# A two-layer decoder trunk on one core: projection weights split into a high and a low part by DMA

## The chip, the cores and the metric

The kernel runs on one core of a Trainium2 chip. The metric is device time in microseconds of that core, lower is better; a separate profiled execution gives the trace from which the engines' work is read. The engines are PE (matmuls), PEld (its weight loads), DVE (VectorE), ACT (ScalarE), POOL (GpSimd) and SP (SyncE, which here only issues DMAs).

## The reference

Two layers, each a pre-norm mixer, on a sequence of 1024 rows of width 1024, all in float32:

```python
for l in range(DEPTH):                                  # 2
    ada = silu(c) @ w_ada[l] + b_ada[l]
    shift, scale, gate = jnp.split(ada, 3, axis=-1)
    h = rmsnorm(x, norm_g[l]) * (1.0 + scale[:, None, :]) + shift[:, None, :]
    p = h @ w_in[l]                                     # 1024 x 9224
    mq, mk, mv, mo, mz, mi, mf, rq, rk, rv, rz = split_cols(p)
    ...
    y = jnp.concatenate([y_m, y_r], axis=-1) @ w_out[l] # y_m, y_r: 4 mLSTM and 4 retention heads of 256
    x = x + gate[:, None, :] * y
return rmsnorm(x, final_g)
```

Most of the arithmetic is the product with w_in: 72 column groups of 128 (and eight gate columns) per layer, then the product with w_out.

## The kernel before, in words

**Three products for one.** A float32 operand is held as two float32r tiles, a rounded high part and the rest, the low part. Each product is three matmuls, high x high, high x low and low x high (`mm3`, lines 145 to 147). Every operand therefore has to be split: `split_to` (lines 621 and 622) lets ACT copy the tile into the high part, which rounds it, and then an engine (POOL unless another is named) subtracts the high part from the tile and writes the low part.

**The projections.** `hT` holds the normalised input, transposed, split, in 8 groups of 128 rows of k and two halves of 512 columns of the sequence. `proj_units` (line 363) does one 128-column projection in four units: for each half of the sequence, k 0 to 3 and then k 4 to 7, 12 matmuls each; after a half its PSUM bank is evacuated by ACT and DVE. `v_path` (line 579) does the 256 columns of a head's v in eight row tiles, each of which runs through all eight k. `load_w` (line 353) brings the weights: `load_w_raw` (line 338) has SP issue a DMA of 256 KB into a `raw` tile of 128 x 512 (four k of 128 columns, or two k of 256), and `split_w` (line 348) splits it into a `wH` and a `wL` tile. A 128-column projection takes two such blocks, a v takes four. The `raw` tiles share four buffers, `wH` and `wL` six each.

**What does not go through `load_w`.** The first three projections of each layer (`first`, line 1194) have their own loads: in layer 0 tiles of another pool, in layer 1 `load_w_raw` and `split_w` (line 1187). The v of head 0 and the gate columns (`v0_raw`, line 419, and `v0_split`) load eight raw tiles of 128 x 256 per layer through the same four `raw` buffers. In layer 0 four of these loads are issued before the hand-written order of the first stage (`script`, line 1208) begins, and each of the others when the split of the tile four before it has been written down. The output stage (`OutLoads`, line 955) draws w_out in 64 pieces per layer through `raw`, `wH` and `wL`, and with them the normalised head outputs (`yr`) and the gates (`gr`). The adaLN sums draw w_ada through `raw` too (`ada_rows`, line 254).

**What sets the order.** PE runs in the order in which the program is written, and so does every engine in the first stage of layer 0. Elsewhere a planner orders each engine's queue at build time, by its own estimate of when an instruction can start; on the chip each queue is run strictly in that order. While the projections run, `tick` (line 124) advances generators that write the attention of earlier heads between units of projections: scores (split into `sH` and `sL`, the low part by POOL), values, state updates, and the normalisation, whose power -0.5 is taken by POOL (lines 899 and 904).

Of the kernel before, what the change touches and what calls it, by code (L numbers as in the profile page):

```python
# [77 lines left out]


@with_exitstack  # L80
def tile_hybrid_trunk(ctx, tc, x, xt, c, positions, w_ada, b_ada, norm_g, w_in, conv_w, conv_b,
                      b_igate, b_fgate, gn_m, gn_r, w_out, final_g, consts, out):
    nc = tc.nc
    V, A, G, PE, Q = nc.vector, nc.scalar, nc.gpsimd, nc.tensor, nc.sync
# [169 lines left out]
    def ada_rows(l, c0, accs):  # L254
        acc = bt()
        accs.append(acc)
        prev = None
        for k in range(KT + 1):
            raw = None
            if k < KT:  # L260
                raw = wt("raw", 512, 4)
                Q.dma_start(raw, w_ada[l, k * P:(k + 1) * P, c0:c0 + 512])
            if k == 1:
                V.tensor_scalar(acc, prev, cact[:, 0:1], None, ALU.mult)
            elif k > 1:
# [18 lines left out]
    def gate_rows(l, res):  # L284
        for half in range(2):
            accs = []
            yield from ada_rows(l, 2 * D + half * 512, accs)
            brow = wt("th", 512, 5)
            Q.dma_start(brow[0:1, :], b_ada[l, 2 * D + half * 512:2 * D + (half + 1) * 512].unsqueeze(0))
            yield 1  # L290
            acc = accs[0]
            V.tensor_tensor(acc[0:1, :], acc[0:1, :], brow[0:1, :], ALU.add)
            yield 1
            a2 = (wt("wH", 512, 6, F32R), wt("wL", 512, 6, F32R))
# [40 lines left out]
            V.tensor_scalar(hf, pt, gsh[l][:, 0, k:k + 1], gsh[l][:, 1, k:k + 1], ALU.mult, ALU.add)  # L335
        return hf

    def load_w_raw(src, c0, n):
        kk = 512 // n
        raws = []  # L340
        for p in range(KT // kk):
            raw = wt("raw", 512, 4)
            Q.dma_start(raw.rearrange("p (a b) -> p a b", a=kk),
                        src[p * kk * P:(p + 1) * kk * P, c0:c0 + n].rearrange("(a p) b -> p a b", p=P))
            raws.append(raw)
            yield raw

    def split_w(raw, n, eng=G):
        wH, wL = wt("wH", 512, 6, F32R), wt("wL", 512, 6, F32R)
        split_to((wH, wL), raw, eng)  # L350
        return [(wH[:, a * n:(a + 1) * n], wL[:, a * n:(a + 1) * n]) for a in range(512 // n)]

    def load_w(src, c0, n):
        res = []
        for raw in load_w_raw(src, c0, n):
            res += split_w(raw, n)
        return res

    def half_block(pt, w, hT, half, k0, k1):
# [57 lines left out]
        return gr  # L417

    def v0_raw(l, k):
        raw = wt("raw", 512, 4)[:, 0:HD]  # L420
        Q.dma_start(raw, w_in[l, k * P:(k + 1) * P, OFF_MV:OFF_MV + HD])
        return raw

# [143 lines left out]
    def ocol(hg, m):  # L567
        return OFF_MO + hg * HD + m * P

    def gate_path(l, hg, hT, res, m0=0, m1=2, z0=True):  # L570
        for m in range(m0, m1):
            if m or z0:
                w = load_w(w_in[l], zcol(hg, m), P)
                yield from proj_units(w, hT, z_evac(res, m, None if hg < 4 else gdr[l][hg]))
            if hg < 4:
                w = load_w(w_in[l], ocol(hg, m), P)
                yield from proj_units(w, hT, o_evac(res, m, gdr[l][hg]))

    def v_path(l, hg, hT, gt, vs):
        h, ml = hg % 4, hg < 4  # L580
        w = load_w(w_in[l], (OFF_MV if ml else OFF_RV) + h * HD, HD)
        for half in range(2):
            for jj in range(2):
                j = half * 2 + jj
                pt = ps_p()
                for tt in range(2):
                    o = pt[:, tt * HD:(tt + 1) * HD]
                    ts = slice(jj * CH + tt * P, jj * CH + (tt + 1) * P)
                    for k in range(KT):
                        mm3(o, (hT[k][half][0][:, ts], hT[k][half][1][:, ts]), w[k], k == 0, k == KT - 1)  # L590
                    if tt == 0:
                        yield
                vs.append(v_split(hg, gt, pt, j))
                yield
# [85 lines left out]

    def qk_ml(l, hg, which, hT, gt, kt, res):
        for m in range(2):
            w = load_w(w_in[l], (OFF_MK if which else OFF_MQ) + hg * HD + m * P, P)
            halo = wt("halo", 3, 2)

            def evac(half, pt):
                acc = conv_silu(l, hg, which, m, half, pt, halo)
                if not which:
                    q_split(acc, res[m], half)
                    return  # L690
                t2 = (bt(F32R), bt(F32R))
                split_to(t2, acc)
                res[m][half] = t2
                k_store(acc, l, hg, m, half)
                if m:
                    for j in ((0, 1), (2,))[half]:
                        launch(k_rows(l, hg, j, kt, gt), 1)

            yield from proj_units(w, hT, evac)

    def qk_ret(l, h, which, hT, kt, res, cosT, sinT):
        base = (OFF_RK if which else OFF_RQ) + h * HD
        su = []

        def evac0(half, p0):
            s, u = wt("acc", 512, 4), wt("acc", 512, 4)
            V.tensor_tensor(s, p0, cosT[half], ALU.mult)
            V.tensor_tensor(u, p0, sinT[half], ALU.mult)
            su.append((s, u))

        def evac1(half, p1):
            s, u = su[half]
            a, b = wt("th", 512, 5), wt("th", 512, 5)
            V.tensor_tensor(a, p1, sinT[half], ALU.mult)
            V.tensor_tensor(b, p1, cosT[half], ALU.mult)
            V.tensor_tensor(s, s, a, ALU.subtract)  # L716
            V.tensor_tensor(u, u, b, ALU.add)
            for m, src in ((0, s), (1, u)):
                if not which:
# [10 lines left out]
        w = load_w(w_in[l], base, P)  # L730
        yield from proj_units(w, hT, evac0)
        w = load_w(w_in[l], base + P, P)
        yield from proj_units(w, hT, evac1)

    def load_rotary(rot):
# [219 lines left out]
    class OutLoads:  # L955
# [3 lines left out]

        def stage(self, n=1):  # L960
            for half, cc, k in self.todo[:n]:
                raw = wt("raw", 512, 4)
                Q.dma_start(raw, w_out[self.l, k * P:(k + 1) * P, cc * 512:(cc + 1) * 512])
                wH, wL = wt("wH", 512, 6, F32R), wt("wL", 512, 6, F32R)
# [217 lines left out]
    for l in range(DEPTH):  # L1182
# [1 line left out]
        gp = [[None, None], [None, None]]  # L1184
        wf = [[], [], []]
        if l > 0:
            gens = [load_w_raw(w_in[l], col, P) for col in (zcol(0, 0), ocol(0, 0), zcol(0, 1))]
# [18 lines left out]
        if l == 0:  # L1206
# [10 lines left out]
            for step in script.split():  # L1217
# [55 lines left out]
                        vrw.append(v0_raw(0, n + 4))  # L1273
                elif what == "W":
                    i, p = arg
                    wsp[i, p] = wt("wH", 512, 6, F32R), wt("wL", 512, 6, F32R)
# [25 lines left out]
        run_units(proj_units(load_w(w_in[l], ocol(0, 1), P), hT, o_evac(gp, 1, gdr[l][0])))  # L1302
        gp1 = [[None, None], [None, None]]
        run_units(proj_units(load_w(w_in[l], zcol(1, 0), P), hT, z_evac(gp1, 0)))
        gb = []
        gcol = gsh[0][:, 0, :]
        for hg in range(8):
# [65 lines left out]
        hT = nhT  # L1373


_INS = ['x', 'xt', 'c', 'positions', 'w_ada', 'b_ada', 'norm_g', 'w_in', 'conv_w', 'conv_b', 'b_igate', 'b_fgate',
        'gn_m', 'gn_r', 'w_out', 'final_g']
_OUTS = [((1, T, D), 'float32')]

# [23 lines left out]
```

## Time and profile before

| what | value |
|---|---|
| device time, median of 2 runs | 2300.2 us (2299.34 to 2301.05) |
| profiled execution, span from first to last instruction | 2298.7 us |
| PE busy | 2269.4 us, 12411 matmuls |
| DVE busy | 1338.7 us |
| ACT busy | 926.5 us |
| POOL busy | 827.5 us |
| bytes moved by DMA | 259.45 MB, 39.8% of the 16 DMA engines' span |
| mean granted clock | 0.999 |

The profile gives the span of the profiled execution, and no time around it; the two timed runs lie 0.6 and 2.4 us above the span. Busy time is the sum of instructions of an engine; the issuing of DMAs is not counted in it. A row of a group of instructions names line, engine, operation, output and inputs, shapes and count, then busy time and mean length in ns, then how long the engine stood idle just before them and what ended most of that. A row of the timeline gives start, length, engine, line, operation and count. A row of a stretch gives length, the busy time of PE, PEld, DVE, ACT and POOL with their instruction counts, the granted clock, the DMA share and GB/s. A row of waits gives who waited for whom, the total, how often, and the longest.

### The profile page before, as it was taken

How to read it: one execution, taken by the hardware profiler on the slowest of the kernel's cores; microseconds unless marked ns; L12 is line 12 of the kernel's file. 1: busy time of each engine (PE TensorE's matmuls, PEld its weight loads, DVE VectorE, ACT ScalarE, POOL GpSimd, SP SyncE). 2: the span in 40 equal slices, each digit the busy share in tenths (PEclk: the TensorE clock that was granted, in tenths of full speed). 3: DMA queues.
4: the chain of work that ended last, by engine and by line, in shares of the span. 5: the costliest groups of instructions: out<-in, count | busy, mean ns of one | idle time of the engine just before them, and what ended most of it. 6: DMA issues, size and time to landing. Idle time of an engine off the chain costs nothing. (4 is left out here: it accounts for less than half of the span.)

```text
span 2298.7 us, 34322 instructions
## 1 busy us (share of the span) xinstructions
PE 2269.4 (99%) x12411; PEld 1953.7 (85%) x12411; DVE 1338.7 (58%) x2821; ACT 926.5 (40%) x1785; POOL 827.5 (36%) x820
## 2 busy tenths in 40 slices
PE   7999999999999999999999999999999999999998
PEld 5888888889988888988888889888898898988886
DVE  7467688556555555585435676555564545556563
ACT  7535433444332323343544454444343323234442
POOL 0343333333333334224562434333334334341313
PEclk9999999999999999999999999999999999999999
DMA  8333333324433533476532323233223233436674
GB/s 258 80 69 94 83 80 82 83 70 115 124 110 87 149 96 79 126 254 212 169 105 67 84 71 82 77 77 79 68 71 98 74 91 88 124 84 205 184 242 125
DMA packets 360246, 259.45 MB, mean 113 GB/s; under 512 B 113266, under 2 KB 297338, under 8 KB 360076
## 3 DMA queue, kind: packets, MB, share of 16 engines
q1 hardware_dynamic: 359932, 257.00, 39.8%
q8 instruction: 97, 1.59, 0.3%
q14 instruction: 73, 0.60, 0.1%
q10 hardware_dynamic: 144, 0.26, 0.0%
HBM read 201.57 MB, written 55.61 MB: 112 GB/s over the span
## 5 line engine op out<-in xcount | busy, mean ns | idle before, releaser
L145 PE MATMUL pp<-b,wH 128*128 128x512 f32 x1824 | 719.6, 395 | 0.0
L146 PE MATMUL pp<-b,wH 128*128 128x512 f32 x1824 | 718.6, 394 | 0.0
L147 PE MATMUL pp<-b,wL 128*128 128x512 f32 x1824 | 717.6, 393 | 0.0
L622 POOL TENSOR_TENSOR wL<-raw,wH 128x512 fp32r<-128x512 f32 x338 | 453.9, 1351 | 542.3 <-ACT wH L621 478.7
L147 PEld LDWEIGHTS pp<-b,wL 128*128 128x128 f32 x1824 | 342.5, 188 | 80.4
L145 PEld LDWEIGHTS pp<-b,wH 128*128 128x128 f32 x1824 | 342.7, 188 | 73.1 <-DVE g L550 0.3
L146 PEld LDWEIGHTS pp<-b,wH 128*128 128x128 f32 x1824 | 342.5, 188 | 72.1 <-issue 0.2
L621 ACT CAST wH<-raw 128x512 fp32r<-128x512 f32 x402 | 245.7, 616 | 310.8 <-PE pp L146 109.9
L145 PE MATMUL pp<-wH,b 128*128 128x256 f32 (+1 forms) x1024 | 303.0, 296 | 0.0
L147 PE MATMUL pp<-wH,b 128*128 128x256 f32 (+1 forms) x1024 | 301.9, 295 | 0.0
L146 PE MATMUL pp<-wL,b 128*128 128x256 f32 (+1 forms) x1024 | 301.9, 295 | 0.0
L622 POOL TENSOR_TENSOR b<-acc,b 128x256 fp32r<-128x256 f32 (+1 forms) x192 | 176.6, 939 | 299.0 <-ACT b L621 287.7
L146 PEld LDWEIGHTS pp<-wL,b 128*128 128x128 f32 x1024 | 192.9, 188 | 5.8
L145 PEld LDWEIGHTS pp<-wH,b 128*128 128x128 f32 x1024 | 192.4, 188 | 6.0 <-DVE g L550 0.3
L147 PEld LDWEIGHTS pp<-wH,b 128*128 128x128 f32 x1024 | 192.7, 188 | 5.7
L639 DVE SCALAR_TENSOR_TENSOR acc<-pp,cols,acc 128x511 f32<-128x511 f32 (+2 forms) x192 | 142.4, 742 | 40.7 <-ACT acc L634 38.8
L621 ACT CAST b<-acc 128x256 fp32r<-128x256 f32 (+1 forms) x192 | 83.8, 476 | 180.7 <-DVE acc L716 129.3
L622 POOL TENSOR_TENSOR sL<-th,sH 128x256 fp32r<-128x256 f32 (+1 forms) x62 | 57.9, 934 | 207.7 <-ACT sH L621 161.9
L643 ACT ACTIVATE th<-acc 128x512 f32<-128x512 f32 x64 | 40.5, 632 | 145.7 <-DVE acc L641 77.9
L621 ACT CAST cH<-cf 128x516 fp32r<-128x516 f32 (+1 forms) x80 | 49.8, 622 | 105.8 <-DVE va L903 55.7
L622 DVE TENSOR_TENSOR wL<-raw,wH 128x512 fp32r<-128x512 f32 x64 | 44.3, 694 | 62.5 <-ACT wH L621 58.7
L145 PE MATMUL pa<-b,b 128*128 128x256 f32 (+1 forms) x256 | 72.3, 283 | 1.8 <-DVE th L787 1.0
(297 smaller groups left out, 3639.2 us busy)
## 6 DMA issues: line engine op xcount, KB each, us to landing
raw<-in_w_in_dram SPq DMA_DIRECT2D x274, 256.0 KB
raw<-in_w_out_dram SPq DMA_DIRECT2D x128, 256.0 KB
gdr<-g SPq DMA_DIRECT2D x64, 256.0 KB
ndr<-zt SPq DMA_DIRECT2D x128, 128.0 KB
raw<-in_w_ada_dram SPq DMA_DIRECT2D x64, 256.0 KB
g<-gdr SPq DMA_DIRECT2D x64, 256.0 KB
acc<-ndr SPq DMA_DIRECT2D x64, 256.0 KB
acc<-kdr SPq DMA_DIRECT2D x192, 64.0 KB
```

The source lines that it names most:

```text
L145: PE.matmul(o, lt[0], rt[0], start=start, stop=False)
L146: PE.matmul(o, lt[0], rt[1], start=False, stop=False)
L147: PE.matmul(o, lt[1], rt[0], start=False, stop=stop)
L621: A.copy(dst[0], src)
L622: eng.tensor_tensor(dst[1], src, f(dst[0]), ALU.subtract)
L639: V.scalar_tensor_tensor(acc[:, d:], pt[:, 0:HALF - d], wcol, acc[:, d:], ALU.mult, ALU.add)
L643: A.activation(th, acc, AF.Tanh, scale=0.5)
```

## The change

`load_w` no longer brings a raw tile. For each block POOL issues a DMA from w_in's block straight into `wH`, a float32r tile, so that the DMA rounds; ACT writes the negated `wH` into `wL`; and POOL issues a second DMA from the same block that adds to `wL`. The result in `wL` is the weight less its high part. The subtraction on POOL and the cast on ACT go for these blocks. For that the host lays w_in out a second time: `w_blk` with 72 column groups, each as two contiguous blocks of 128 x 512, and `w_val` with the v columns of eight heads, each as four. `load_w_raw` (now only for the start of layer 1) reads those blocks as well, still by SP. `wH` and `wL` get seven buffers instead of six, `raw` two instead of four. The loads of w_out, w_ada and the v of head 0 are as they were, but share the two `raw` buffers.

```diff
-                raw = wt("raw", 512, 4)
+                raw = wt("raw", 512, 2)
...
-    def load_w_raw(src, c0, n):
-        kk = 512 // n
-        raws = []
-        for p in range(KT // kk):
-            raw = wt("raw", 512, 4)
-            Q.dma_start(raw.rearrange("p (a b) -> p a b", a=kk),
-                        src[p * kk * P:(p + 1) * kk * P, c0:c0 + n].rearrange("(a p) b -> p a b", p=P))
-            raws.append(raw)
+    def w_block(l, c0, n, p):
+        if n == P:
+            return w_blk[l, (c0 - 8 * (c0 > OFF_I)) // P, p]
+        return w_val[l, (c0 - OFF_MV) // HD if c0 < OFF_I else NH + (c0 - OFF_RV) // HD, p]
+
+    def load_w_raw(l, c0, n):
+        for p in range(KT * n // 512):
+            raw = wt("raw", 512, 2)
+            Q.dma_start(raw, w_block(l, c0, n, p))
             yield raw
 
     def split_w(raw, n, eng=G):
-        wH, wL = wt("wH", 512, 6, F32R), wt("wL", 512, 6, F32R)
+        wH, wL = wt("wH", 512, 7, F32R), wt("wL", 512, 7, F32R)
         split_to((wH, wL), raw, eng)
         return [(wH[:, a * n:(a + 1) * n], wL[:, a * n:(a + 1) * n]) for a in range(512 // n)]
 
-    def load_w(src, c0, n):
+    def load_w(l, c0, n):
         res = []
-        for raw in load_w_raw(src, c0, n):
-            res += split_w(raw, n)
+        for p in range(KT * n // 512):
+            wH, wL = wt("wH", 512, 7, F32R), wt("wL", 512, 7, F32R)
+            G.dma_start(wH, w_block(l, c0, n, p))
+            A.activation(wL, f(wH), AF.Copy, scale=-1.0)
+            G.dma_start(wL, w_block(l, c0, n, p), accum_op=ALU.add)
+            res += [(wH[:, a * n:(a + 1) * n], wL[:, a * n:(a + 1) * n]) for a in range(512 // n)]
         return res
...
     def v0_raw(l, k):
-        raw = wt("raw", 512, 4)[:, 0:HD]
+        raw = wt("raw", 512, 2)[:, 0:HD]
...
+    cols = _np.concatenate([w[:, :, :OFF_I], w[:, :, OFF_I + 8:]], 2).reshape(DEPTH, 2, 4, P, 72, P)
+    vals = _np.concatenate([w[:, :, OFF_MV:OFF_MV + 1024], w[:, :, OFF_RV:OFF_RV + 1024]], 2)
+    laid = {'xt': inputs['x'][0].T, 'w_blk': cols.transpose(0, 4, 1, 3, 2, 5).reshape(DEPTH, 72, 2, P, 512),
+            'w_val': vals.reshape(DEPTH, 4, 2, P, 8, HD).transpose(0, 4, 1, 3, 2, 5).reshape(DEPTH, 8, 4, P, 512)}
```

More of the change, by code (lines that the diff above doesn't have):

```diff
@@ L80, in tile_hybrid_trunk @@
 @with_exitstack
-def tile_hybrid_trunk(ctx, tc, x, xt, c, positions, w_ada, b_ada, norm_g, w_in, conv_w, conv_b,
+def tile_hybrid_trunk(ctx, tc, x, xt, c, positions, w_ada, b_ada, norm_g, w_in, w_blk, w_val, conv_w, conv_b,
                       b_igate, b_fgate, gn_m, gn_r, w_out, final_g, consts, out):
@@ L293, in gate_rows @@
             yield 1
-            a2 = (wt("wH", 512, 6, F32R), wt("wL", 512, 6, F32R))
+            a2 = (wt("wH", 512, 7, F32R), wt("wL", 512, 7, F32R))
             split_to(a2, acc)
@@ L572, in gate_path @@
             if m or z0:
-                w = load_w(w_in[l], zcol(hg, m), P)
+                w = load_w(l, zcol(hg, m), P)
                 yield from proj_units(w, hT, z_evac(res, m, None if hg < 4 else gdr[l][hg]))
             if hg < 4:
-                w = load_w(w_in[l], ocol(hg, m), P)
+                w = load_w(l, ocol(hg, m), P)
                 yield from proj_units(w, hT, o_evac(res, m, gdr[l][hg]))
@@ L580, in v_path @@
         h, ml = hg % 4, hg < 4
-        w = load_w(w_in[l], (OFF_MV if ml else OFF_RV) + h * HD, HD)
+        w = load_w(l, (OFF_MV if ml else OFF_RV) + h * HD, HD)
         for half in range(2):
@@ L682, in qk_ml @@
         for m in range(2):
-            w = load_w(w_in[l], (OFF_MK if which else OFF_MQ) + hg * HD + m * P, P)
+            w = load_w(l, (OFF_MK if which else OFF_MQ) + hg * HD + m * P, P)
             halo = wt("halo", 3, 2)
@@ L728, in evac1 @@
                     launch(k_rows(l, h + 4, j, kt, None), 1)
-        w = load_w(w_in[l], base, P)
+        w = load_w(l, base, P)
         yield from proj_units(w, hT, evac0)
-        w = load_w(w_in[l], base + P, P)
+        w = load_w(l, base + P, P)
         yield from proj_units(w, hT, evac1)
@@ L961, in stage @@
             for half, cc, k in self.todo[:n]:
-                raw = wt("raw", 512, 4)
+                raw = wt("raw", 512, 2)
                 Q.dma_start(raw, w_out[self.l, k * P:(k + 1) * P, cc * 512:(cc + 1) * 512])
-                wH, wL = wt("wH", 512, 6, F32R), wt("wL", 512, 6, F32R)
+                wH, wL = wt("wH", 512, 7, F32R), wt("wL", 512, 7, F32R)
                 split_to((wH, wL), raw, G if cc else V)
@@ L1186, in tile_hybrid_trunk @@
         if l > 0:
-            gens = [load_w_raw(w_in[l], col, P) for col in (zcol(0, 0), ocol(0, 0), zcol(0, 1))]
+            gens = [load_w_raw(l, col, P) for col in (zcol(0, 0), ocol(0, 0), zcol(0, 1))]
             for _ in range(2):
@@ L1275, in tile_hybrid_trunk @@
                     i, p = arg
-                    wsp[i, p] = wt("wH", 512, 6, F32R), wt("wL", 512, 6, F32R)
+                    wsp[i, p] = wt("wH", 512, 7, F32R), wt("wL", 512, 7, F32R)
                     A.copy(wsp[i, p][0], rw[i][p])
@@ L1301, in tile_hybrid_trunk @@
             head_cols(1, load_head_rows(1))
-        run_units(proj_units(load_w(w_in[l], ocol(0, 1), P), hT, o_evac(gp, 1, gdr[l][0])))
+        run_units(proj_units(load_w(l, ocol(0, 1), P), hT, o_evac(gp, 1, gdr[l][0])))
         gp1 = [[None, None], [None, None]]
-        run_units(proj_units(load_w(w_in[l], zcol(1, 0), P), hT, z_evac(gp1, 0)))
+        run_units(proj_units(load_w(l, zcol(1, 0), P), hT, z_evac(gp1, 0)))
         gb = []
@@ L1373, in tile_hybrid_trunk @@
         hT = nhT
-_INS = ['x', 'xt', 'c', 'positions', 'w_ada', 'b_ada', 'norm_g', 'w_in', 'conv_w', 'conv_b', 'b_igate', 'b_fgate',
+_INS = ['x', 'xt', 'c', 'positions', 'w_ada', 'b_ada', 'norm_g', 'w_in', 'w_blk', 'w_val', 'conv_w', 'conv_b', 'b_igate', 'b_fgate',
         'gn_m', 'gn_r', 'w_out', 'final_g']
@@ L1387 @@
     arrays, args = {}, []
+    w = inputs['w_in']
+    cols = _np.concatenate([w[:, :, :OFF_I], w[:, :, OFF_I + 8:]], 2).reshape(DEPTH, 2, 4, P, 72, P)
+    vals = _np.concatenate([w[:, :, OFF_MV:OFF_MV + 1024], w[:, :, OFF_RV:OFF_RV + 1024]], 2)
+    laid = {'xt': inputs['x'][0].T, 'w_blk': cols.transpose(0, 4, 1, 3, 2, 5).reshape(DEPTH, 72, 2, P, 512),
+            'w_val': vals.reshape(DEPTH, 4, 2, P, 8, HD).transpose(0, 4, 1, 3, 2, 5).reshape(DEPTH, 8, 4, P, 512)}
     for name in _INS:
-        a = _np.ascontiguousarray(inputs['x'][0].T if name == 'xt' else inputs[name])
+        a = _np.ascontiguousarray(laid[name] if name in laid else inputs[name])
         arrays[f"in_{name}_dram"] = a
```

## The prediction

> **What bounds the kernel now.** I read the page's head first, then the busy time by stretches, then PE's own waits.
>
> ```profile
> span 2298.7 us, 34322 instructions
> PE 2269.4 (99%) x12411; PEld 1953.7 (85%) x12411; DVE 1338.7 (58%) x2821; ACT 926.5 (40%) x1785; POOL 827.5 (36%) x820
> q1 hardware_dynamic: 359932, 257.00, 39.8%
> ```
>
> ```profile
> 0.00:58.00 58.00, 41.16 (x199) 32.55 (x200) 41.64 (x90) 41.17 (x77) 4.96 (x12) 1.00 0.80 256
> 58.00:115.00 57.00, 57.00 (x347) 50.27 (x346) 24.32 (x57) 32.27 (x62) 19.86 (x24) 1.00 0.31 81
> ...
> 1552.00:1725.00 173.00, 173.00 (x1036) 153.47 (x1035) 97.41 (x246) 71.33 (x145) 57.29 (x63) 1.00 0.28 72
> ...
> 2184.00:2299.00 115.00, 107.24 (x462) 86.46 (x461) 52.59 (x84) 41.41 (x77) 27.39 (x26) 0.98 0.61 183
> ```
>
> ```profile
> PE pp L1263 <- DMA b<-in_w_ada_dram: 8.7, 1, 8.7
> ...
> PE pa L855 <- DVE cL L622: 2.1, 3, 1.2
> PE pa L145 <- DVE th L787: 1.0, 1, 1.0
> ```
>
> PE is idle 2298.7 - 2269.4 = 29.3 us in all. Of that, 58.00 - 41.16 = 16.8 lie in the first stretch and 115.00 - 107.24 = 7.8 in the last, and neither stretch holds a weight load that the change turns into a POOL DMA. Some 4.7 us are left. The granted clock is 1.00 almost throughout. So 4.7 us is the most that any relief of POOL, ACT or DMA can give, and the question is only what PE loses. Two matmul rates set the clock for the rest:
>
> ```profile
> 600.24 0.28 PE L145 MATMUL pp<-wH,b 128*128 128x256 f32 x1
> ...
> 601.67 0.28 PE L145 MATMUL pp<-wH,b 128*128 128x256 f32 x1
> ...
> 602.73 0.39 PE L145 MATMUL pp<-b,wH 128*128 128x512 f32 x1
> ...
> 605.52 0.40 PE L145 MATMUL pp<-b,wH 128*128 128x512 f32 x1
> ```
>
> Each pair of rows is twelve matmuls apart. A quarter of a 128-column projection (four k, three products) is 2.79 us, so such a projection is 11.2 us and uses two blocks, one per 5.58 us. On 256 columns twelve matmuls take 1.43 us.
>
> **The change part by part.**
>
> ```profile
> L622 POOL TENSOR_TENSOR wL<-raw,wH 128x512 fp32r<-128x512 f32 x338 | 453.9, 1351 | 542.3 <-ACT wH L621 478.7
> L621 ACT CAST wH<-raw 128x512 fp32r<-128x512 f32 x402 | 245.7, 616 | 310.8 <-PE pp L146 109.9
> ...
> raw<-in_w_in_dram SPq DMA_DIRECT2D x274, 256.0 KB
> ```
>
> ```profile
> L343 SPq DMA_DIRECT2D raw<-in_w_in_dram x274: 367/379/1297, 66.7 to 2042.7; - x137
> ```
>
> ```profile
> 677.34 0.72 POOL L904 TENSOR_TENSOR rsd<-va,mhalf 128x1 f32<-128x1 f32 x1 [6.73 <-DVE va L903]
> ```
>
> *POOL.* Of the 274 block loads, six (start of layer 1) stay as they are; 268 lose POOL's subtraction: 268 x 1.351 = 362 us off 827.5, leaving 465. Each gains two DMAs issued by POOL, 536. No POOL DMA is in this trace. Bounds for one issue: 0.38 us, SP's for the same transfer, and 1.35 us, POOL's full pass over such a tile. I take 0.72 us, POOL's instruction with hardly any data. POOL then has 465 + 386 = 851 us (669 to 1189 by the bounds): it is not relieved, and not near the span.
>
> *ACT.* 268 casts become 268 negated copies of equal shape; I take the same 0.616 us, so nothing. What ends its waits changes: it waits for the first DMA's landing, where it had a raw tile loaded long before. SP loses 268 issues, off the path.
>
> *DMA engines.* In 58:115 the queues were busy 0.31 x 57 = 17.7 us for 81 GB/s x 57 us = 4.6 MB, about 1.0 us per 256 KB, mostly of w_in, whose rows of 128 columns are 512 bytes. Loads of w_out, with rows as long as the new blocks, had a stretch to themselves:
>
> ```profile
> 1067.14:1079.38 12.24, 12.24 (x54) 9.89 (x53) 5.98 (x10) 4.69 (x8) 2.42 (x2) 1.00 0.26 86
> ```
>
> 0.26 x 12.24 = 3.2 us for 1.05 MB is 0.80 us per load. An accumulating load costs at least that and, with the target read too and each passage counted fully, 2.4; I take 1.6. Sum: 39.8% of 2298.7 is 915 us; minus 268 x 1.0, plus 268 x 2.4, is 1290 us, 56%. Hidden by PE.
>
> *The time from a free slot to usable weights.* It was ACT plus POOL, 2.0 us, on a tile already there. Now it is landing, negation, landing:
>
> ```profile
> 609.85 1.62 SPq L343 DMA_DIRECT2D raw<-in_w_in_dram  x2
> ```
>
> ```profile
> 612.71 0.62 ACT L621 CAST wH<-raw 128x512 fp32r<-128x512 f32 x1 [3.74 <-DMA raw<-in_w_in_dram]
> ```
>
> Landing took 2.86 us from the issue. 2.86 + 0.62 + 2.86 + 0.8 (the accumulating extra) = 7.1 us. Seven slots give the time for it. The tightest case is the fourth v block: it takes the slot of the first block two projections earlier, free after three quarters (8.4 us), and is first read at 22.3 + 2.1 = 24.4 us. 16 us against 7.1: weights themselves come in time, and this costs nothing. If that cover were gone, each v (14 of them) would lose what exceeds 16 us.
>
> *POOL's in-order queue.* The second DMA waits for ACT's copy, which waits for the first. If the two follow each other, a block holds POOL for 2.86 + 0.62 + 0.72 = 4.2 us. Queued behind are the q and k splits, the power for the norms and sL, the low part of the scores, and PE reads sL:
>
> ```profile
> 654.14 1.01 POOL L622 TENSOR_TENSOR sL<-th,sH 128x384 fp32r<-128x384 f32 x1 [0.77 <-ACT sH L621]
> ...
> 685.95 1.00 POOL L622 TENSOR_TENSOR sL<-th,sH 128x384 fp32r<-128x384 f32 x1
> ```
>
> ```profile
> L845 PE MATMUL pa<-b,sL x3: 280/283/284, 658.4 to 658.7; 128*128 128x256 f32 x3
> ```
>
> ```profile
> L147 PE MATMUL pa<-b,sL x5: 280/281/287, 690.9 to 707.0; 128*128 128x256 f32 x5
> ```
>
> The cover is 658.4 - 655.15 = 3.25 us for a head's first chunk and 690.9 - 686.95 = 3.95 for its last (the two between have over 10): 32 tight places in 16 heads. A block stands open on POOL 268 x 4.2 / 2298.7 = 49% of the time, so 16 places meet one, and at worst exceed the cover (mean 3.6) by 0.6 us: 0 to 10 us. I take 5.
>
> *Raw buffers, four to two.* At the start of each layer the eight raw v tiles of head 0 go through them, and in layer 0 that order is written out by hand for four.
>
> ```profile
> 58.52 6.72 SPq L421 DMA_DIRECT2D raw<-in_w_in_dram  x4
> ...
> 1195.96 2.91 SPq L421 DMA_DIRECT2D raw<-in_w_in_dram  x4
> ```
>
> ```profile
> 1197.99 0.41 ACT L621 CAST b<-raw 128x256 fp32r<-128x256 f32 x1 [2.29 <-DMA raw<-in_w_in_dram]
> ```
>
> ```profile
> 61.87 0.75 POOL L622 TENSOR_TENSOR b<-raw,b 128x256 fp32r<-128x256 f32 x1
> ```
>
> ```profile
> 63.62 0.40 ACT L621 CAST b<-raw 128x256 fp32r<-128x256 f32 x1
> ...
> 67.58 0.81 ACT L1242 ACTIVATE b<-b,gsh 128x512 fp32r<-128x512 f32 x1
> ```
>
> ```profile
> 68.44 0.50 PE L1200 MATMUL pp<-b,wH 128*128 128x512 f32 x1
> ```
>
> Such a tile lands 1197.99 - 1195.96 = 2.0 us after its issue. In layer 0 the fourth tile can start only when the second is split, at 62.6, and lands at 64.6, where ACT wanted it at 63.62: 1.0 us. The next four repeat that every second tile (landing, cast 0.40, split 0.75, behind six small loads that SP now issues after the fourth); I get 0.8 to 1.0 more. ACT passes it on, for its last hT pieces end (68.39) just as PE reads them (68.44): +2.0 us, between 0 and 4. In layer 1 the last four tiles come one landing later in pairs; PE's first v unit needs the eighth some 0.8 us before it would be there: +0.8.
>
> *The output stage* draws 128 w_out pieces through the same two buffers, one per 2.79 us of PE. A buffer's round is landing 2.86, cast 0.62, split 1.35 at most: 4.8 us for two pieces' 5.58. With the gate and norm rows loading too, landings are longer:
>
> ```profile
> 2100.97 4.70 DMA g<-gdr
> 2105.76 0.63 DVE g L972
> 2106.48 5.40 DMA acc<-ndr
> ```
>
> Then DVE does the split (0.69), so up to 5.40 + 0.62 + 0.69 = 6.7 us a round, 1.1 too long, over eight rounds of a half: 9 us, against five weight slots ahead, 14 us. I take nothing.
>
> **Sum** against the profiled span: 2298.7 + 5 + 2.0 + 0.8 = 2306.5. The median of the runs, 2300.2, is 1.5 above that span, so 2308 us.
>
> **The rivals.** *POOL held by two blocks at once.* If the planned order puts blocks back to back, or the first DMA's wait for a slot (ACT's 109.9 us of waiting for PE moves to POOL) adds to the hold, it is 8.4 us: 16 places x (8.4 - 3.6) = 77 us, and with the 2.8 us of the starts 2380. It decides (46 us, 2%) from holds of 46 / 16 + 3.6 = 6.5 us. For it: the long chains, and v's four blocks in a row; against: POOL is empty 64% of the time, so an order that leaves room is easy. *Two raw buffers starve the output stage*: with landings of 8 us a round is 9.3, 3.7 too long, 30 us in a half less the 14 ahead, four halves: +62, and with the starts 2365. It decides from landings of 6.0 us; the longest shown is 5.4. *Slow issue or slow accumulation.* POOL becomes the bound at (2298.7 - 465) / 536 = 3.4 us an issue; at 4.0 it is +310 us, 2610. The DMA engines become it where a pair costs 5.6 us, against 2.4 taken. The nearest rows are far below both. The Trainium skill, page "SBUF — State Buffer", section "Who interferes with whom", speaks against the change: a copy, cast or scalar operation of VectorE in its two-port mode locks GpSimd out. Its section "A bandwidth-pool intuition that's wrong" tells of a DMA issued from GpSimd that took about 3100 ns under such an operation and 620 alone, since its descriptors could not be written. By that figure POOL would hold an estimated 465 + 536 x 3.1 = 2127 us. The row that bears on it:
>
> ```profile
> L611 DVE CAST b<-eH 128x4 fp32r<-128x4 f32 x32 | 11.6, 361 | 0.0
> ```
>
> That is the costliest such DVE group, 11.6 of 1338.7 us, so I give that case little. *It is hidden altogether*, or wins back PE's small waits: 2300.2 less 0 to 4.7, 2296 to 2300.
>
> **How the numbers follow.** The forecast, with doses of the rivals that stay within 2%, 0.56; all hidden, or a small gain, 0.19; POOL held 0.12; output stage 0.07; slow issue or accumulation 0.06. The likeliest gives 2308. The range 2294 to 2370 holds the first two and the output stage, 0.82; the likeliest one's own, by the bounds of its terms (0 to 10, 0 to 4, 0.8), is 2301 to 2315. Within 2% (2254 to 2346; that much a measurement of this kernel can tell) are the first two, 0.74 after 0.01 for faster, which the 29.3 us of idle PE all but exclude; slower is the rest, 0.25.
>
> **What would show it.** POOL's subtraction count falls to 70 and POOL DMA issues number 536, at 0.4 to 1.35 us. PE's busy time stays near 2269; its waits stay under 20 us beyond the old, on sL and on hT at the start. DMA share near 0.56. I am wrong if PE waits for wL or wH in projections, if waits on sL exceed 50 us, or if the accumulating DMA lands over 8 us after its issue.

## The result and the profile after

The changed kernel takes 2393.2 us (2393.09 to 2393.37, two runs) against 2300.2: a ratio of 1.0403 with an interval of 1.0373 to 1.0433, 93 us slower, above the range of the prediction. The lines named below are those of the changed kernel: L358 is the DMA that rounds into wH, L359 ACT's negation, L360 the accumulating DMA, and L626 and L627 are the two halves of `split_to`.

The head of the page after, and its two busiest queues (packets, MB, share of the 16 DMA engines):

```profile
span 2391.7 us, 34381 instructions
...
PE 2308.5 (97%) x12411; PEld 1974.3 (83%) x12411; DVE 1269.7 (53%) x2821; ACT 927.9 (39%) x1785; POOL 864.1 (36%) x1088
...
q0 software_dynamic: 77184, 140.54, 30.9%
q1 hardware_dynamic: 230460, 186.73, 27.3%
```

PE does the same 12411 matmuls, but is idle for 2391.7 - 2308.5 = 83.2 us where it was 29.3, and its busy time is 39.1 us longer. 53.9 + 39.1 is the 93. No other engine that computes is busy for more than 53% of the span, and the DMA engines are at 58%.

Where the idle time lies is seen by cutting both executions alike: the first 80 us, the middle, the last 170 us. A row gives the stretch, its length, the busy time of PE, PEld, DVE, ACT and POOL, then the granted clock, the DMA share and GB/s. Before:

```profile
0.00:80.00 80.00, 63.16 (x334) 51.98 (x335) 49.95 (x110) 56.69 (x114) 19.85 (x32) 1.00 0.72 224
80.00:2129.00 2049.00, 2044.02 (x11363) 1769.88 (x11362) 1207.07 (x2574) 805.95 (x1554) 758.50 (x746) 1.00 0.37 103
2129.00:2299.00 170.00, 162.24 (x717) 131.87 (x716) 81.65 (x139) 63.92 (x119) 49.20 (x43) 0.99 0.63 182
```

And after:

```profile
0.00:80.00 80.00, 58.42 (x256) 45.70 (x257) 46.75 (x100) 53.94 (x107) 19.28 (x34) 0.94 0.77 224
80.00:2222.00 2142.00, 2096.18 (x11524) 1809.04 (x11523) 1154.78 (x2614) 817.54 (x1575) 798.87 (x1014) 0.99 0.58 133
2222.00:2392.00 170.00, 153.91 (x634) 119.60 (x632) 68.13 (x109) 56.38 (x105) 45.98 (x40) 0.96 0.57 162
```

PE's idle time goes from 16.8 to 21.6 us at the start, from 5.0 to 45.8 in the middle and from 7.8 to 16.1 at the end. Most of what is new lies in the middle. And the granted clock, which was 1.00, 1.00 and 0.99, is lower in all three. What PE waited for, after (total, times, longest):

```profile
PE pa L860 <- ACT cH L626: 13.2, 10, 3.5
PE pa L145 <- ACT nd L864: 9.1, 2, 4.5
...
PE pp L1209 <- DVE b L1257: 7.4, 4, 2.8
PE pa L850 <- ACT sH L626: 6.5, 3, 3.5
PE pa L860 <- DVE cL L627: 6.2, 6, 1.5
...
PE pa L850 <- POOL sL L627: 2.0, 5, 0.6
```

But for L1209, which belongs to the start, these are steps of the attention (the state cH and cL, the scores sH, the evacuation nd), and they come from ACT or from DVE right behind it. No wait for wL or wH of a projection is in the whole list, and sL costs 2.0 us. So it isn't the weights of the projections that are late; it is what ACT does for the attention. The groups and waits of ACT and POOL say why:

```profile
L359 ACT ACTIVATE wL<-wH 128x512 fp32r<-128x512 f32 x268 | 167.5, 630 | 502.8 <-DMA wH<-in_w_blk_dram 376.9
L360 POOL DMA_DIRECT2D wL<-in_w_blk_dram x212 | 190.8, 924 | 393.9 <-ACT wL L359 277.9
...
L358 POOL DMA_DIRECT2D wH<-in_w_blk_dram x212 | 130.7, 617 | 265.9 <-PE pp L147 254.3
...
wH<-in_w_blk_dram POOLq DMA_DIRECT2D x212, 256.0 KB, 3.4
wL<-in_w_blk_dram POOLq DMA_DIRECT2D x212, 256.0 KB, 4.5
```

```profile
ACT wL L359 <- DMA wH<-in_w_blk_dram: 376.9, 122, 11.4
...
ACT wH L626 <- DMA raw<-in_w_out_dram: 124.6, 71, 5.5
ACT wL L359 <- DMA wH<-in_w_val_dram: 89.2, 31, 6.1
```

The negation takes 630 ns, as the cast did, but ACT stands still 376.9 + 89.2 = 466 us in front of it, waiting for the first DMA to land (3.4 us in the median). ACT is busy 39% and can afford 466 us; what is queued behind cannot. One place of it, in the timeline:

```profile
577.74 1.52 POOL L358 DMA_DIRECT2D wH<-in_w_val_dram  x1
...
579.71 0.39 ACT L626 CAST sH<-th 128x256 fp32r<-128x256 f32 x1
...
585.16 0.63 ACT L359 ACTIVATE wL<-wH 128x512 fp32r<-128x512 f32 x1 [5.06 <-DMA wH<-in_w_val_dram]
...
585.69 0.58 ACT L553 ACTIVATE th<-pp 128x512 f32<-128x512 f32 x1
586.17 0.47 ACT L864 ACTIVATE nd<-pa,wd 128x258 f32<-128x258 f32 x1
586.21 0.88 POOL L360 DMA_DIRECT2D wL<-in_w_val_dram  x1 [4.61 <-ACT wL L359]
...
586.69 0.58 PE L145 MATMUL pa<-b,b 128*128 128x256 f32 x1 [4.53 <-ACT nd L864]
```

ACT reaches the negation at 580.1 and stands for 5.06 us. The evacuations th and nd stand behind it and show no wait of their own once it is through; nd reads out the PSUM tile that PE writes next, and PE is idle for 4.53 us until then. POOL has meanwhile stood 4.61 us for ACT. The same place in stretches (the granted clock is the third number from the end):

```profile
580.00:584.70 4.70, 2.16 (x10) 1.41 (x8) 1.08 (x2) 0.10 (x1) 1.35 (x2) 1.00 1.08 280
584.70:591.50 6.80, 4.81 (x16) 4.29 (x17) 4.91 (x10) 2.73 (x5) 1.78 (x2) 0.50 0.77 212
591.50:598.00 6.50, 6.50 (x37) 5.58 (x36) 5.50 (x17) 2.10 (x4) 1.20 (x2) 1.00 0.59 173
```

The DMA engines are full in the first (1.08 by this view, 280 GB/s; loads of w_ada go beside the weights), which is the likely reason that this landing took over 7 us. And for 6.8 us, from within the gap on, the clock is 0.50: the gap is paid a second time. How much that is shows at the end of another such stretch, from 229.7 to 233.1 us; the last two rows are at full clock again:

```profile
231.64 0.42 PE L145 MATMUL pa<-b,sH 128*128 128x258 f32 x1
...
231.85 0.42 PE L146 MATMUL pa<-b,sH 128*128 128x258 f32 x1
...
233.12 0.28 PE L146 MATMUL pa<-b,b 128*128 128x258 f32 x1
...
233.24 0.28 PE L147 MATMUL pa<-b,b 128*128 128x258 f32 x1
```

A matmul starts every 0.21 us at half clock and every 0.12 at full. The execution has sixteen stretches at half clock, 70 us in all (before: one of 4.3 us at the very end, without a matmul), and PE was busy in 56 us of them. 56 x (1 - 0.12 / 0.21) is some 24 us lost, most of the 39 us by which PE's busy time grew; the rest is not traced here.

### The profile page after: what moved, and what is told of

It reads as the page before. It is cut to its first block, busy times and chain, and to the rows that moved or that the text cites. A ratio compares the mean times of both kernels' runs of the same rounds, so it can differ in the third digit from the quotient of the medians.

```text
span 2391.7 us, 34381 instructions
## 1 busy us (share of the span) xinstructions
PE 2308.5 (97%) x12411; PEld 1974.3 (83%) x12411; DVE 1269.7 (53%) x2821; ACT 927.9 (39%) x1785; POOL 864.1 (36%) x1088
## 3 DMA queue, kind: packets, MB, share of 16 engines
q0 software_dynamic: 77184, 140.54, 30.9%
## 5 line engine op out<-in xcount | busy, mean ns | idle before, releaser
L147 PE MATMUL pp<-b,wL 128*128 128x512 f32 x1824 | 720.2, 395 | 0.0
L147 PEld LDWEIGHTS pp<-b,wL 128*128 128x128 f32 x1824 | 344.1, 189 | 80.2
L359 ACT ACTIVATE wL<-wH 128x512 fp32r<-128x512 f32 x268 | 167.5, 630 | 502.8 <-DMA wH<-in_w_blk_dram 376.9
L360 POOL DMA_DIRECT2D wL<-in_w_blk_dram x212 | 190.8, 924 | 393.9 <-ACT wL L359 277.9
L147 PE MATMUL pp<-wH,b 128*128 128x256 f32 (+1 forms) x1024 | 303.2, 296 | 1.1 <-DVE b L981 1.1
L627 POOL TENSOR_TENSOR b<-acc,b 128x256 fp32r<-128x256 f32 (+1 forms) x192 | 185.1, 1015 | 131.6 <-ACT b L626 130.9
L358 POOL DMA_DIRECT2D wH<-in_w_blk_dram x212 | 130.7, 617 | 265.9 <-PE pp L147 254.3
L147 PEld LDWEIGHTS pp<-wH,b 128*128 128x128 f32 x1024 | 193.0, 189 | 8.2 <-DVE b L981 2.5
L627 POOL TENSOR_TENSOR wL<-raw,wH 128x512 fp32r<-128x512 f32 x70 | 95.2, 1363 | 149.9 <-ACT wH L626 116.1
L626 ACT CAST wH<-raw 128x512 fp32r<-128x512 f32 x134 | 82.5, 617 | 167.0 <-DMA raw<-in_w_out_dram 124.6
L627 POOL TENSOR_TENSOR sL<-th,sH 128x256 fp32r<-128x256 f32 (+1 forms) x62 | 61.2, 987 | 173.2 <-ACT sH L626 139.9
L626 ACT CAST b<-acc 128x256 fp32r<-128x256 f32 (+1 forms) x192 | 83.2, 474 | 85.4 <-DVE acc L721 46.1
L360 POOL DMA_DIRECT2D wL<-in_w_val_dram x56 | 51.2, 940 | 118.3 <-ACT wL L359 90.0
```

What stands on the lines that cost most here:

```text
L147: PE.matmul(o, lt[1], rt[0], start=False, stop=stop)
L358: G.dma_start(wH, w_block(l, c0, n, p))
L359: A.activation(wL, f(wH), AF.Copy, scale=-1.0)
L360: G.dma_start(wL, w_block(l, c0, n, p), accum_op=ALU.add)
L626: A.copy(dst[0], src)
L627: eng.tensor_tensor(dst[1], src, f(dst[0]), ALU.subtract)
```

## The experiments

Theory A: two things cost. The negation and the second DMA stand in two in-order queues, ACT's and POOL's, ahead of the landing they wait for, and hold what is queued behind; and two raw buffers are too few at the starts and in the output stage. In the first four runs A had ACT's queue alone as the cause in the middle, and up to the eighth it still had ACT's wait as what PE feels; the form given here is that of the ninth run on. Against it stand a rival that the raw buffers are all of it (B), one that POOL's held queue is all of the chain's cost (D, in the first eight runs), and one that the doubled reading and the issues cost by themselves (C). From the ninth run D is this last one, as the expectations there say. Each time is the median of the runs of that kernel, each ratio is to the kernel before beside it (2299.4 to 2300.0 in the four groups), with its interval.

**Layout alone.** The blocks of w_in laid out by the host, everything else as before: SP loads, ACT casts, POOL subtracts, four raw buffers and six slots.

```diff
-        for p in range(KT * n // 512):
...
-            G.dma_start(wH, w_block(l, c0, n, p))
-            A.activation(wL, f(wH), AF.Copy, scale=-1.0)
-            G.dma_start(wL, w_block(l, c0, n, p), accum_op=ALU.add)
...
+        for raw in load_w_raw(l, c0, n):
+            res += split_w(raw, n)
```

> The weights in blocks, but split as before (SP loads a raw tile, ACT casts, POOL subtracts), with the four raw and six weight buffers of before. Theory A (ACT's in-order queue waits for the landing of the first DMA, PE then waits for ACT's attention steps, and each such gap is followed by a stretch at half clock): no such wait is left, 2290 to 2303 us. Rival B (two raw buffers): also as before. Rival C (the new layout or the DMA engines' load itself): stays above 2320.

Measured 2298.8 us, ratio 0.9997 [0.9988, 1.0007]. The layout neither costs nor brings anything that this measurement can tell.

**The old split with two raw buffers.** The same edit, with the buffers of the changed kernel (two raw, seven slots).

> As e1, but with the changed kernel's two raw and seven weight buffers, so every weight block goes through the two raw tiles as well. Of the 93 us that the change cost, the trace of the changed kernel shows about 32 at the two starts (v of head 0) and in the last output stage: idle PE plus half of the stretches at half clock there. Theory A: about 2332, and none of the waits of attention. Rival B, that the raw buffers are the whole cause: about 2393.

Measured 2343.0 us, 1.0188 [1.0173, 1.0203]: nearer to A. Here all weights pass through the two buffers, which they don't in the changed kernel, so the 44 us are probably more than the buffers' part there.

**Negation on POOL.**

```diff
-            A.activation(wL, f(wH), AF.Copy, scale=-1.0)
+            G.tensor_scalar(wL, f(wH), -1.0, None, ALU.mult)
```

> The changed kernel with the negated copy on POOL instead of ACT: ACT no longer waits for a weight DMA at all, and POOL's own queue holds for the landing instead. Theory A: the attention gaps ended by ACT (cH, nd, sH) go, the two starts and the end stay, 2325 to 2350. Rival D (the hold of POOL's queue is what PE feels, as the prediction priced it): POOL is held at least as long as now plus its own copy, 2400 or more.

Measured 2547.7 us, 1.1074 [1.1055, 1.1092]. Theory A's expectation failed by far, and rival D's number was met. POOL's waits in this kernel, the two of the negation:

```profile
POOL wL L359 <- DMA wH<-in_w_blk_dram: 446.2, 152, 7.2
...
POOL wL L359 <- DMA wH<-in_w_val_dram: 99.3, 38, 4.9
```

The 545 us of standing still were not gone; they had moved from ACT's queue to POOL's, where the next DMAs and the splits of q and k stand behind them; PE waits 37.8 us for such splits (`PE pa L147 <- POOL b L627`), a wait that the changed kernel doesn't have. So the wait is bad in POOL's queue too. How much of the 248 us it is stays open, for POOL takes 1.6 us for a negation where ACT took 0.63 and is 1278 us busy, 414 more than in the changed kernel.

**No chain.** The second DMA loads the block rounded, as the first does, and nothing is negated. The low part of the weights is left out.

```diff
-            A.activation(wL, f(wH), AF.Copy, scale=-1.0)
-            G.dma_start(wL, w_block(l, c0, n, p), accum_op=ALU.add)
+            G.dma_start(wL, w_block(l, c0, n, p))
```

> The changed kernel without the negated copy, and with the second DMA a plain rounding load into the low tile: both DMAs go out without waiting for each other, on the same queue and of nearly the same bytes. It leaves out the forming of the low part (the low tile holds the high part again). Theory A: no engine waits for the landing of a weight, 2325 to 2340 (the starts and the end stay). Rival C (contention of the DMA engines, or POOL's issuing): still above 2370.

Measured 2329.0 us, 1.0129 [1.0114, 1.0144], as A had it: 64 of the 93 us go with the chain, with the same bytes and the same number of issues. But with the waits go 268 instructions of ACT, and an issue takes POOL 0.54 us where the accumulating one took 0.92; which of these it is, the run does not say.

**Four raw buffers, six slots**, with the chain as changed; then **the same without the chain** (low part left out).

```diff
-            raw = wt("raw", 512, 2)
+            raw = wt("raw", 512, 4)
...
-            wH, wL = wt("wH", 512, 7, F32R), wt("wL", 512, 7, F32R)
+            wH, wL = wt("wH", 512, 6, F32R), wt("wL", 512, 6, F32R)
```

> The changed kernel with the buffers of before: four raw, six of each weight tile. Theory A with its share for the buffers (30 of the 93 us are the two raw buffers at the starts and the end, as e4 without the chain showed; 64 are the waits of the chain in the middle): 2355 to 2372, with the attention gaps as in the changed kernel. Rival B': a seventh slot is worth more than raw buffers: 2393 or above.

> e4 (both DMAs from POOL, none waiting for the other, no low part formed) with four raw buffers and six weight slots. If the account is complete (buffers 30, chain 64, nothing else), 2297 to 2305, though the DMA engines still move the 70 MB more and POOL still issues 536 DMAs. If bytes or issuing cost something by themselves: 2310 or more.

Measured 2350.8 us, 1.0226 [1.0210, 1.0241], some 4 us better than A had it, and 2296.1 us, 0.9983 [0.9973, 0.9992]. The second says that 268 blocks read twice and 536 issues on POOL cost next to nothing: what leaving out ACT's and POOL's work on these blocks may give back is 4.7 us at most, by the idle time of PE before. The rival of traffic falls.

**Each queue's wait alone.** ACT's negation without the second DMA (what is left out is adding the weights to the low part), and a second DMA on POOL that copies wH to wL without ACT (low part left out), both with two raw buffers.

```diff
-            G.dma_start(wL, w_block(l, c0, n, p), accum_op=ALU.add)
```

> The changed kernel without the second DMA: ACT's negated copy still waits for the landing, but nothing on POOL waits for ACT's copy. It leaves out the adding of the weights to the low part. Theory A (ACT's wait is what PE feels): 2370 to 2395. Rival D (POOL's wait for ACT is): 2325 to 2345, as e4.

```diff
-            A.activation(wL, f(wH), AF.Copy, scale=-1.0)
-            G.dma_start(wL, w_block(l, c0, n, p), accum_op=ALU.add)
+            G.dma_start(wL, f(wH))
```

> The changed kernel with the low tile copied by a second POOL DMA from the high tile just landed, and no copy on ACT: POOL waits for the landing before each second DMA, ACT for nothing of the weights' before PE. It leaves out the forming of the low part. Theory A: 2325 to 2345. Rival D: 2370 or more. Between the two (2345 to 2370 in both e7 and e8): each queue's wait costs for itself.

Measured 2344.4 us, 1.0196 [1.0179, 1.0213], and 2331.9 us, 1.0139 [1.0124, 1.0154]. For the second, theory A's number came and rival D's failed. For the first, D's came and theory A's failed: ACT stands 361.5 + 84.1 us there, nearly what it does in the changed kernel, and it costs 15 us over the kernel without the chain, not 41 or more. POOL's wait alone costs 3. The whole chain costs 64, so 46 us come only when one queue waits for the other. A place in the changed kernel shows how:

```profile
224.45 0.63 ACT L359 ACTIVATE wL<-wH 128x512 fp32r<-128x512 f32 x1 [6.11 <-DMA wH<-in_w_blk_dram]
...
225.51 0.87 POOL L360 DMA_DIRECT2D wL<-in_w_blk_dram  x1 [6.33 <-ACT wL L359]
...
226.08 0.84 POOL L768 TENSOR_SCALAR_AFFINE_SELECT dm<-dm 128x128 f32<-128x128 f32 x2
...
226.72 0.40 ACT L769 ACTIVATE dm<-dm,COL 128x128 f32<-128x128 f32 x1 [1.64 <-POOL dm L768]
...
229.51 0.62 ACT L626 CAST cH<-cf 128x516 fp32r<-128x516 f32 x1 [1.33 <-DVE qd L899]
...
230.18 1.23 PE L860 MATMUL pa<-cH,b 128*128 128x258 f32 x4 [3.47 <-ACT cH L626]
```

ACT stands 6.11 us for a landing; POOL stands 6.33 us for ACT; POOL's masks for the scores stand behind that; ACT, free again, waits 1.64 us for the masks; the evacuations and the state come after them, and PE loses 3.47 us.

**The negation later in the queue.** If place is the cause, moving the negation must give the time back. The planner orders ACT's queue by when it believes a landing will be; here it is told not to order the negation before the tenth product (`mm3`) after the slot's last use. Work, bytes, buffers and DMAs stay. `late` is a dependency that orders and does not wait.

```diff
...
-            A.activation(wL, f(wH), AF.Copy, scale=-1.0)
+            neg = A.activation(wL, f(wH), AF.Copy, scale=-1.0)
+            if len(held) - 7 in last:
+                mm = mms[min(last[len(held) - 7] + 10, len(mms) - 1)]
+                tc.add_manual_dep(neg.ins, mm.ins.name, NOSYNC, reason="late")
...
```

`held` lists the blocks in order and 7 is the number of slots, so block `len(held) - 7` is the one that had the slot before; `last` gives the last product that used it, and `mms` the first matmul of each product. The lines that keep these lists are left out.

> The kernel after the change, with nothing changed but the place of ACT's negation in ACT's queue: the planner is told not to order it before the tenth product that follows the last use of the block that held the slot, about 6 us, so it comes some two ACT instructions (about 3 us) later; the second DMA moves back with it in POOL's queue. Work, bytes and buffers are as in the kernel after. Theory A (the negation and the second DMA stand in two in-order queues before the landing, and what is queued behind them waits): ACT's waits for wH fall from 377 and 89 us to 150 to 300 us together, the gaps of PE in the middle of the kernel fall from 38 us to 15 to 28, and the time is 2350 to 2378. Rival D (the chain costs by its work, its bytes and its two issues, wherever it stands): no change, 2388 to 2398. Rival W (the weights have no cover left): PE begins to wait for wL in the projections and the time is 2395 to 2430.

Measured 2341.8 us, 1.0181 [1.0166, 1.0196]: 51 of the chain's 64 us are back, more than theory A asked for. In the traces the 268 negations stand 2.05 places later in ACT's order in the mean, and the second DMAs, which follow them, 0.66 places later in POOL's; so what is moved is the chain's place in both queues, by little. ACT's negation (L366 in this kernel) now stands far less, and so does PE in the middle:

```profile
L366 ACT ACTIVATE wL<-wH 128x512 fp32r<-128x512 f32 x268 | 165.8, 628 | 229.4 <-DMA wH<-in_w_blk_dram 182.6
```

```profile
80.00:2171.00 2091.00, 2074.73 (x11490) 1795.55 (x11489) 1142.58 (x2605) 818.44 (x1571) 794.07 (x1011) 1.00 0.58 135
```

2091 - 2074.7 is 16.3 us of idle time in the middle against 45.8, and the clock there is 1.00 again, to two places. The DMA share, 0.58, is that of the changed kernel.

**Later still (sixteen products), and the first with four raw buffers.**

> The same with sixteen products in place of ten, about 10 us after the slot came free, so the negation comes some four ACT instructions (about 6 us) later than in the kernel after the change. Theory A: ACT's waits for wH fall below 150 us, PE's gaps in the middle below 15 us, and the time is 2330 to 2360, near the 2329 of the kernel with no chain at all. Rival D: 2388 to 2398. Rival W: the chain is now as long as the 16 us that cover it, PE waits for wL at many blocks, 2380 to 2450.

> The kernel with four raw buffers and six slots (2350.8) with the negation moved as in the kernel with ten products. Theory A: the middle gaps fall from 37 us to 10 to 25 and the time is 2310 to 2338, on the way to the 2296 of the same kernel without the chain. Rival D: 2347 to 2356. Rival W, with one slot fewer: 2350 to 2390.

Measured 2344.1 us, 1.0197 [1.0182, 1.0212], and 2308.3 us, 1.0040 [1.0025, 1.0055]. The second, a little under theory A's range, gives back 43 of the 55 us that the chain costs with four raw buffers. The first is in theory A's range but gains nothing over ten products, and a new wait of PE appears in it, which rival W named at a much higher price:

```profile
PE pp L153 <- DMA wL<-in_w_val_dram: 8.4, 7, 1.6
```

So the cover of the weights, for a v 16 us by the prediction, is indeed not endless, and a negation may come too late as well as too early. With six slots that is so at ten products already, as this row of the second kernel shows. The changed kernel and the one without a chain have no such wait; the changed chain with six slots has one, of 5.3 us.

```profile
PE pp L153 <- DMA wL<-in_w_val_dram: 7.7, 3, 4.7
```

**Rounding by DMA, subtraction from a raw tile.** No DMA depends on another any more: SP loads the raw tile, a POOL DMA rounds the same block into wH, and POOL subtracts; four raw buffers. Then the subtraction kept behind the tenth product, on POOL and on DVE.

```diff
-        for p in range(KT * n // 512):
...
+        for p, raw in enumerate(load_w_raw(l, c0, n)):
...
-            A.activation(wL, f(wH), AF.Copy, scale=-1.0)
-            G.dma_start(wL, w_block(l, c0, n, p), accum_op=ALU.add)
+            G.tensor_tensor(wL, raw, f(wH), ALU.subtract)
```

> Four raw buffers and six slots; SP loads the raw tile of each block, a POOL DMA rounds the same block into wH, and POOL subtracts as before the change, so ACT has neither cast nor negation for these blocks and no DMA depends on another. Theory A (only the chain through ACT and POOL costs, not the second read of the weights nor 268 issues on POOL): 2295 to 2302, the time before or a little below. Rival D (bytes and issues cost): 2310 to 2350. Rival P (POOL, with its 268 subtractions back and 268 issues more, holds up its other subtractions): 2305 to 2330.

> The kernel whose POOL subtracts from the raw tile after a POOL DMA has rounded the block (2335.1), with POOL's subtraction kept in the plan behind the tenth product after the slot's last use, so it comes about 2 us later in POOL's queue; work, bytes and issues are the same. Theory A (what costs is that a step stands in an in-order queue ahead of the landing it waits for, here POOL behind its own DMA): POOL's unnamed and DMA waits ahead of the subtraction fall from about 290 us to below 150, PE's gaps in the middle fall from 29 us to below 15, and the time is 2300 to 2318. Rival P (POOL has more to do than before the change, 971 us with its issues, and holds its other subtractions whatever the order): 2328 to 2340.

> The same with the late subtraction on DVE in place of POOL (268 of about 0.7 us, 188 us more on DVE, 350 us less on POOL). Theory A: no queue waits long for a landing, 2296 to 2312. Rival P would have it better than on POOL by 15 us or more whatever the place; rival V (DVE, at 58% busy and in order, now holds the evacuations): 2320 to 2360.

Measured 2335.1 us, 1.0155 [1.0138, 1.0172]; 2323.5 us, 1.0104 [1.0089, 1.0119]; 2297.2 us, 0.9992 [0.9982, 1.0001]. Theory A's numbers failed for the first two. The first lies in rival D's range and 5 us above P's; the third, with the same bytes and issues, lets D fall. POOL stands here too, in front of the subtraction. For the largest part the profile shows no releaser and writes "issue"; what the subtraction still needs there is the wH that POOL's own DMA brings, by inference:

```profile
POOL wL L359 <- issue: 204.9, 83, 4.7
```

With the subtraction moved back (L366) the same row reads:

```profile
POOL wL L366 <- issue: 30.9, 27, 3.1
```

That returns 12 of 36 us. PE's idle time in the middle falls from 28.8 to 21.1 us, not below 15, and 9.9 us of PE's waits there are now for the wL of the late subtraction. 26 more go only when POOL loses the work (it was 970 us busy with its issues; with DVE subtracting, 640). So the place counts, and so does what is left on POOL; whether that is its work or what it still waits for, these runs don't part. The last kernel takes 188 us off POOL and 143 off ACT against the kernel before, and is no faster that this measurement can tell. That agrees with the 4.7 us that the prediction gave as the most to be won.

The six kernels that differ in the chain and in the buffers alone, in us:

| buffers | no chain | chain, negation later | chain as changed |
|---|---|---|---|
| four raw, six slots | 2296.1 | 2308.3 | 2350.8 |
| two raw, seven slots | 2329.0 | 2341.8 | 2393.2 |

Down a column is the price of the buffers, 33, 34 and 42 us; the number of raw buffers and that of slots change together there and were not tried apart. Along a row, the chain where it is placed well costs 12 or 13 us, and its place 43 or 51 more.

## Why the prediction was wrong, step by step

*The bound* was right: PE is the bound, and no kernel's median came below 2296.

*POOL's load* was right: 864 us against 851, with issues of 0.62 and 0.92 us where 0.72 was taken for both. *The DMA engines* too: 58% against 56%, and hidden, as the kernel without a chain and with four raw buffers shows.

*ACT* is the first step that failed: "268 casts become 268 negated copies of equal shape; I take the same 0.616 us, so nothing. What ends its waits changes". The duration held (0.630). But the change of what ends the wait was named and then priced at nothing, without asking what stands behind it in ACT's queue: the evacuations, the scores and the state. ACT stood 466 us, and moving the negation, with the DMA that follows it, gives back 51 us.

*POOL's in-order queue* was priced, but only for POOL's own hold on sL, at 5 us. PE's waits on POOL's sL are 2.0 us, and POOL's wait alone costs 3: the size was right and the place did not matter. What was missed is the loop: the two waits cost 15 and 3 us alone and 64 together. POOL's hold was taken as 4.2 us with ACT answering at once; ACT answers when its own queue lets it, and what it does next waits for POOL. The rival "POOL held by two blocks at once" gave 2380, close to the time, by sL, which was not it; that closeness is luck. None of the three signs of being wrong that the prediction named was seen (PE has no wait for wL or wH in projections, 2.0 us on sL, and the accumulating DMA lands 4.5 us after its issue in the median), for none of them looked at ACT. What did fail was the expectation beside them that PE's waits stay under 20 us beyond the old: they grew by 54.

*The raw buffers* are a mis-sized term: 2.0 + 0.8 us for the starts and nothing for the output stage, against 33 to 42 us measured. At the start PE's idle time grew by 4.7 us and at the end by 8.3; with four raw buffers and the chain both are as before but for 1.2 us (16.5 and 9.0 against 16.8 and 7.8). The output stage's sum was a round of 6.7 us for 5.58 with 14 us ahead, "I take nothing"; but ACT stands 124.6 us for raw tiles of w_out, where it did 14.2 before, shown by this row of the kernel before:

```profile
ACT wH L621 <- DMA raw<-in_w_out_dram: 14.2, 12, 2.5
```

So the rival that the output stage starves was probably right in kind, at a half to two thirds of the 65 us that it named with the starts; how the 33 to 42 us divide among the places was not tried apart.

*The clock* was left out. The prediction read it as 1.00 and kept it there, so each microsecond of a gap was priced as one. Some 24 of the 93 us are matmuls at half clock beside the new gaps.

*The weights in time* was right: PE never waits for those of the projections in the changed kernel. What stays open is the last 12 or 13 us of a chain that is placed well. With six slots 7.7 us of it are PE's waits for the wL of a v, shown above. With seven there is no such wait; ACT stands 211 us there still (182.6 of it in the row above), which may be it, as may ACT's 268 instructions and the longer issues, which the kernel without a chain doesn't have. That wasn't tried apart.

## What to carry to other kernels

When a step between two DMAs is given to a compute engine, the landing becomes a wait in that engine's in-order queue. Price it by what is queued behind it, on that engine and on every engine that then waits for it, not by the engine's busy share: ACT had 60% of its time free, and still the place of one instruction in its queue, with the DMA that follows it, cost 51 us. Try the place first: the same instructions ordered two ACT instructions later were worth more here than the buffers.

## What the runs showed of the hardware

A gap in PE's work can cost more than its length. Of the 17 gaps of 1.4 us or more after the first 21.5 us of the changed kernel, 15 have 3.4 or 6.8 us at a granted clock of 0.50 beside them, begun within 2.5 us of the gap's end (one stretch serves two gaps). The shortest of the 15 is 1.45 us; one of 1.87 us and one of 2.02 us had none. The Trainium skill, page "TensorE: Matmul & The Clock Gate", section "Why this matters for your kernels", asks for "No PE-idle gaps >~3µs between matmul bursts"; here gaps of half that length already had a stretch of lowered clock beside them. Its section "What's actually happening" speaks of a free-running window of about 3.4 us, and the length of the slow stretches agrees with that.

A DMA of 256 KB that POOL issues took POOL 0.62 us when it rounds and 0.92 us when it accumulates, and landed 3.4 and 4.5 us after its issue in the median. 140.54 MB on that queue, in the kernel without a chain and with four raw buffers, cost no time that could be measured (2296.1 us).
